# Attention heads in pairs on TensorE: score products that alternate between the row halves of the array, value products between its column halves

## The chip, the cores and the metric

One core of a Trainium2 chip runs the whole program. TensorE (PE, with its weight loads PEld) multiplies, VectorE (DVE) and ScalarE (ACT) do the elementwise work, GpSimd (POOL) builds a few bias tiles, SyncE (SP) issues the weight DMAs. The metric is the device time of one execution in microseconds, lower is better. The profile is of one execution.

## The reference

Four layers over 256 tokens of width 1024, all in float32. Layer 1 mixes pooled channels with causal attention (8 heads of 64), layer 2 is a gated linear recurrence; both are followed by a convolutional feed-forward net. Layers 3 and 4 each have three attention branches over the same tokens, merged by gates, then a feed-forward net and a per-layer embedding. Cut to the attentions:

```python
# layer 1: 8 heads, causal, ALiBi distance (256 tokens are one block, so topk == 0)
logit = einsum('bhqd,bhkd->bhqk', q, k) * scale - slopes * dist      # masked where dist < 0
out = einsum('bhqk,bhkd->bhqd', softmax(logit), v)
# layers 3 and 4
o_mla  = softmax(q @ k.T * scale) @ v                    # 8 heads, q and k 96 wide, v 64 wide
a      = softmax(s[:, 0]) - lam * softmax(s[:, 1])       # 4 heads, two maps each, 64 wide
o_diff = rms_norm(a @ v)                                 # v 128 wide
o_win  = softmax_with_sink(q @ k.T, |q - k| <= 128) @ v  # 8 query heads on 2 key heads, 64 wide
```

## The kernel before

All 256 tokens stay in SBUF as two tiles of 128 tokens; weights stream in chunks of up to 1 MB (three buffers), and ACT and DVE cut each chunk into two exact halves (`hi`, line 258, and `lo`, line 259). The large products run in three passes over these halves (`mm3`, lines 275 to 277); they are the "main products" below, and take nearly all of TensorE. Attention itself is computed in plain float32: each such matmul shows as two MATMUL records, each with its own weight load.

The order of instructions on each engine comes from a list scheduler: it places every instruction by its dependencies and its own estimates, so main products of other work (the gates, the merge) are placed between the steps of a head. Each engine then runs its list in order, and waits for a semaphore where an operand is late.

One head goes through this chain. Scores: two matmuls of 256 columns, one for each half of the queries, into a bank of tag S (two buffers; lines 478 and 479 in layer 1, line 827 else). Softmax: DVE adds a bias and takes the maximum (line 842 or 846), ACT takes the exponential and its sum (line 850), DVE the reciprocal (line 854), ACT normalises (line 859). Transposes on TensorE into a bank of tag T (line 486 or 807), ACT copies them out (line 488 or 809). Value product: two accumulating matmuls with a 64-column weight into half of a bank of tag O (one buffer; lines 490 and 491, or 974 in `pv64`). Two heads share such a bank, one in partitions 0 to 63 and one in 64 to 127, and lines 307 and 308 read it when both are in.

The heads of layer 1, of the differential branch and of the window branch are 64 wide, and two of them lie above each other in one tile: their score matmuls use rows 0 to 63 or rows 64 to 127 of the array. MLA scores use 96 rows. Before, the code finishes one head of a pair ahead of the next; in the differential branch it takes both maps of a head (m = 0 and 1, the same row half) and then the other head:

```python
for e in range(2):                                     # diff
    rr = slice(e * 64, e * 64 + 64)
    for m in range(2):
        sp = self.scores(qk[m][rr, :S], qk[m][rr, S:])
        es.append(self.softmax(sp, FULL, bias))
```

Of the kernel before, what the change touches and what calls it, by code (L numbers as in the profile page):

```python
# [19 lines left out]
P = 128  # L20
S = 256
# [17 lines left out]
# ---------------------------------------------------------------- host: layout only  # L39
# [157 lines left out]
# ---------------------------------------------------------------- device  # L197
class InOrder:
    """An engine whose instructions stay behind those traced before them on it."""
# [9 lines left out]
class Net:  # L209
# [11 lines left out]
    # ---- tiles  # L221
# [22 lines left out]
    # ---- weight stream  # L244
# [27 lines left out]
    # ---- products, three passes over exact halves  # L272
# [6 lines left out]
    def tm_block(self, banks, n, xh, xl, nk, per):  # L279
        """banks[t][:, :n] = x[t] @ W[:, n columns], W in chunks of `per` k tiles."""  # L280
        for k0 in range(0, nk, per):
            wh, wl = self.chunk(per, n)
            for t in range(2):
                for k in range(per):
                    kk = k0 + k
                    self.mm3(banks[t][:, :n], xh[:, kk, t * P:t * P + P], xl[:, kk, t * P:t * P + P],
                             wh[:, k, :], wl[:, k, :], kk == 0, kk == nk - 1)

    def tm_wide(self, banks, xh, xl, kk, last):
        """adds two k tiles into banks[t][n] (1024 columns)."""  # L290
        wh, wl = self.chunk(2, D)
        for n in range(2):
            for t in range(2):
                for k in range(2):
                    self.mm3(banks[t][n][:, :], xh[:, k, t * P:t * P + P], xl[:, k, t * P:t * P + P],
                             wh[:, k, n * 512:n * 512 + 512], wl[:, k, n * 512:n * 512 + 512],
                             kk + k == 0, last and k == 1)
# [12 lines left out]
    # ---- small arithmetic  # L310
    def rsqrt(self, m, n, out=None):
        """1/sqrt of m [P, n] (m > 0)."""
        v = self.nc.vector
        i = self.t([P, 16], "ty", I32)
        v.tensor_scalar(i[:, :n], m.bitcast(I32), -0.5, float(0x5F3759DF), op0=ALU.mult, op1=ALU.add)
        y = i[:, :n].bitcast(F32)
        t = self.t([P, 16], "ty")
        for it in range(3):
            r = self.t([P, 16], "ty") if it < 2 or out is None else out
            v.tensor_tensor(out=t[:, :n], in0=y, in1=y, op=ALU.mult)  # L320
            v.scalar_tensor_tensor(t[:, :n], t[:, :n], -0.5, m, op0=ALU.mult, op1=ALU.mult)
            v.scalar_tensor_tensor(r[:, :n], t[:, :n], 1.5, y, op0=ALU.add, op1=ALU.mult)
            y = r[:, :n]
        return y
# [6 lines left out]
    # ---- residual stream  # L331
# [5 lines left out]
    def norm(self, gi, banks=None, update=None):  # L337
        """Adds banks to x. Leaves halves of the transpose of x * gain, and 1/rms of x
        per token in self.r [P, 2]."""
# [30 lines left out]
    def norm_rows(self):  # L370
        """self.rb [P, S]: 1/rms of the tokens along the free axis."""
        nc = self.nc
        dg = self.t([P, 2, P], "w2")
        pb = self.bank("T")
        for t in range(2):
            nc.scalar.activation(dg[:, t, :], self.ident, AF.Copy, scale=self.r[:, t:t + 1])
            nc.tensor.matmul(pb[:, t * P:t * P + P], self.ones, dg[:, t, :], start=True, stop=True)
        self.rb = self.t([P, S], "rb")
        nc.scalar.activation(self.rb, pb[:, :S], AF.Copy)
# [6 lines left out]
    # ---- head norms in token-major  # L386
    def headnorm(self, z, nh, d):
        """rms-normalises the heads of z [P, 2, nh*d] in place."""
# [21 lines left out]
    # ---- start  # L410
# [19 lines left out]
    def vprod(self, a, b, s):  # L430
        """a * b * s of per-partition vectors."""
        r = self.t([P, 1], f"vp{self.n}")
        self.vec_o.scalar_tensor_tensor(r, a, s, b, op0=ALU.mult, op1=ALU.mult)
        return r

    # ---- block A, layer 0: pooling and causal attention
    def pool_attn(self):
# [33 lines left out]
        for c in range(4):  # L471
            ob = self.bank("O")
            for e in range(2):
                h = 2 * c + e
                r0 = e * 64
                sp = self.bank("S")
                q, k = qT[r0:r0 + 64, c, :], kT[r0:r0 + 64, c, :]
                nc.tensor.matmul(sp[:, 0:P], q[:, 0:P], k[:, 0:P], start=True, stop=True)
                nc.tensor.matmul(sp[:, P:384], q[:, P:S], k, start=True, stop=True)
                bias = self.t([P, 384], "qk")  # L480
                nc.gpsimd.tensor_scalar(bias, causal, -(2.0 ** -(h + 1)), None, op0=ALU.mult)
                s, r = self.softmax(sp, spans, bias)
                self.normalise(s, spans, r)
                pt = self.bank("T")
                for j in range(3):
                    nc.tensor.transpose(pt[:, j * P:j * P + P], s[:, j * P:j * P + P], self.ident)
                pT = self.t([P, 384], "pT")
                nc.scalar.activation(pT, pt[:, :384], AF.Copy)
                vc = slice(h * 64, h * 64 + 64)
                nc.tensor.matmul(ob[r0:r0 + 64, 0:S], v[:, 0, vc], pT[:, 0:S], start=True, stop=False)  # L490
                nc.tensor.matmul(ob[r0:r0 + 64, P:S], v[:, 1, vc], pT[:, S:384], start=False, stop=True)
            self.split(ah[:, c, :], al[:, c, :], ob[:, :S])
# [27 lines left out]
    # ---- feed-forward nets  # L520
    def conv(self, src, wname, bname, j, taps, shifts):
        """depthwise convolution along tokens of src [P, S]."""
# [12 lines left out]
    def fm_first(self, xh, xl):  # L535
        """the first two pairs, k tiles 0-3 of all before k tiles 4-7."""
# [16 lines left out]
    def times_r(self, z, src):  # L553
        """z [P, 2, S] = two banks' or one bank's tiles times 1/rms of the tokens."""
# [56 lines left out]
    # ---- block A, layer 1: gated linear recurrence  # L611
    def softplus(self):
        """-4 and 2 times softplus(-lambda) per channel [P, NR]."""
# [24 lines left out]
    def after(self, ins, group):  # L638
        """ins is issued behind all of group (same engine)."""
# [4 lines left out]
    def rglru(self, gi):  # L644
# [20 lines left out]
        for jp in range(5):  # L665
# [3 lines left out]
            for e in range(2):  # L669
# [5 lines left out]
                # r = (1 + tr) / 2, i = (1 + ti) / 2, w = 4 softplus (1 + tr) = -log a  # L675
# [7 lines left out]
        # sqrt(1 - a^2) = (1 + a) sqrt(tanh(w / 2))  # L683
# [18 lines left out]
    # ---- block B  # L702
# [52 lines left out]
    def layer_scalars(self, i):  # L755
        """minus lambda of the differential attention, rope tables with gains, gain products."""
# [29 lines left out]
    def rope(self, a1, a2, n, shape):  # L786
        """rotates a1, a2 in place."""
# [13 lines left out]
    def transpose4(self, p):  # L801
        """p [P, 2(t), 256 keys] -> [P keys, 2(key block), 256 queries] in SBUF."""
# [9 lines left out]
    def qk_T(self, q, k, d, gain):  # L812
        """q, k: per t APs [P tokens, d] -> [d, q 256 | k 256]."""
# [9 lines left out]

    def scores(self, qT, kT):
# [3 lines left out]
        return sp  # L828

# [5 lines left out]
    def softmax(self, sp, spans, bias=None, sink=None):  # L835
        """exp(scores + bias - max) [P, 512] and 1/sums [P, 2]; sink: (value, -value)."""
# [61 lines left out]
    def mla_heads(self, ch, cl, kr, skr):  # L898
        nc = self.nc
        v_ = nc.vector  # L900
        # queries
# [22 lines left out]
        # keys and values  # L924
# [28 lines left out]
    def mla(self, q4, k4, v):  # L953
# [3 lines left out]
        for cc in range(4):  # L957
            ob = self.bank("O")
            for e in range(2):
                h = 2 * cc + e  # L960
                qk = self.qk_T([q4[:, t, h, :] for t in range(2)], [k4[:, t, h, :] for t in range(2)], 96, self.gm)
                sp = self.scores(qk[:96, :S], qk[:96, S:])
                s, r = self.softmax(sp, FULL)
                self.pv64(ob, e * 64, s, r, v[:, :, h * 64:h * 64 + 64])
# [3 lines left out]
    def pv64(self, ob, r0, s, r, v):  # L968
        """ob[r0:r0+64, queries] = (s / sums) @ v, transposed."""
        nc = self.nc  # L970
        self.normalise(s, FULL, r)
        pT = self.transpose4(s)
        for kb in range(2):
            nc.tensor.matmul(ob[r0:r0 + 64, :S], v[:, kb, :], pT[:, kb * S:kb * S + S], start=kb == 0, stop=kb == 1)  # L974
# [13 lines left out]
    def diff(self, z, v):  # L988
        nc = self.nc
        o = self.t([P, 2, 512], "w4")  # L990
        for hp in range(2):
            qk = []
            for m in range(2):
                cs = slice((2 * m + hp) * P, (2 * m + hp) * P + P)
                qk.append(self.qk_T([z[0][:, t, cs] for t in range(2)], [z[1][:, t, cs] for t in range(2)], P, self.gd))
            for e in range(2):
                h = 2 * hp + e
                rr = slice(e * 64, e * 64 + 64)
                es = []
                bias = self.bias(self.dist, self.slopes(8 + h))  # L1000
                for m in range(2):
                    sp = self.scores(qk[m][rr, :S], qk[m][rr, S:])
                    es.append(self.softmax(sp, FULL, bias))
                (e0, r0), (e1, r1) = es
# [46 lines left out]
    def window(self, i, q, kT, v, oh, ol, heads):  # L1051
        nc = self.nc
        for c in heads:
# [5 lines left out]
            ob = self.bank("O")  # L1059
            for g in range(2):  # L1060
                h = g * 4 + c
                rr = slice(g * 64, g * 64 + 64)
                sp = self.scores(qT[rr, :], kT[rr, :])
                s, r = self.softmax(sp, FULL, self.bias(self.distw, self.slopes(h)),
                                    (self.row(f"sink{i}", 8)[:, h:h + 1], self.negsink[:, h:h + 1]))
                self.pv64(ob, g * 64, s, r, v[:, :, g * 64:g * 64 + 64])
# [12 lines left out]
    def hybrid(self, i, g0):  # L1079
# [54 lines left out]
        # per-layer embedding  # L1134
# [68 lines left out]
```

## Time and profile before

| | |
|---|---|
| median of 3 runs | 1552.79 us (1552.57 to 1553.59) |
| span of the profiled execution | 1551.6 us, 1.2 us under that median |
| TensorE busy | 1532.8 us |
| VectorE / ScalarE busy | 1138.5 us / 941.2 us |
| attention of layer 1 | about 48 to 75 us |
| attention of layers 3 and 4 | about 660 to 803 us and 1140 to 1278 us |

A record of a matmul holds its whole passage through the array, so records overlap and their durations add up to more than the time that they cost: what a group of matmuls costs is read from the starts of the records around it. "Cost of a cluster" below means the time from the start of the last main product ahead of a group to the start of the second main product behind it, less two ordinary pitches of main products.

### The profile page before, as it was taken

The page shows a single profiled execution, that of the slowest core. Times are in us where ns is not written, and L with a number is a line of the kernel's source. Part 1 is how long each engine was busy: PE and PEld are TensorE (multiplying, and loading weights), DVE is VectorE, ACT ScalarE, POOL GpSimd, SP SyncE. Part 2 cuts the span into 40 slices and gives each one's busy share as a digit, 9 for nine tenths or more (in the row PEclk, how much of TensorE's full clock was granted, in tenths as well). Part 3 has the DMA queues.
Part 4 walks back from the last instruction along what each step waited for, and adds up shares of the span by engine and source line. Part 5 has one row for each costly group of instructions (what it writes and reads, how often), then busy time and mean ns, then how long its engine had stood idle before and what let it go on. Part 6 is the DMA issues. An engine that isn't in the chain of part 4 may idle for free.

```text
span 1551.6 us, 25326 instructions
## 1 busy us (share of the span) xinstructions
PE 1532.8 (99%) x10020; PEld 1368.8 (88%) x10020; DVE 1138.5 (73%) x2189; ACT 941.2 (61%) x1675; POOL 51.9 (3%) x45
## 2 busy tenths in 40 slices
PE   8999999999999999999999999999999999999998
PEld 6689999898999998888888999988888889999996
DVE  6559777789897778865767766668885757777666
ACT  6746555685765556756665655566766774655544
POOL 0200000000000000000220000000000210000000
PEclk9999999999999999999999999999999999999999
DMA  8355455435455554533224555544542225455551
GB/s 298 133 178 191 170 192 187 163 136 191 139 214 190 190 178 146 215 132 114 102 103 169 191 191 179 178 173 166 180 179 109 99 86 190 169 186 188 191 188 56
DMA packets 37878, 257.33 MB, mean 166 GB/s; under 512 B 4384, under 2 KB 4768, under 8 KB 8320
## 3 DMA queue, kind: packets, MB, share of 16 engines
q1 hardware_dynamic: 36864, 252.45, 46.0%
q0 software_dynamic: 896, 3.28, 0.7%
q8 instruction: 78, 1.28, 0.3%
q14 instruction: 40, 0.33, 0.1%
HBM read 254.66 MB, written 1.05 MB: 165 GB/s over the span
## 4 chain that ended last, share of the span: by engine, by line
PE 91%; DVE 5%; ACT 2%; issue 1%; DMA 0%; SPq 0%; ACTq 0%; DVEq 0%
PE A L276 14%; PE A L277 13%; PE A L275 13%; PE S L277 6%; PE S L276 6%; PE S L275 6%; PE T L277 6%; PE T L276 5%; PE T L275 5%; PE S L827 2%; PE O L275 2%; PE O L276 2%; PE O L277 2%; PE O L974 2%; DVE lo L259 2%; PE T L807 1%
## 5 line engine op out<-in xcount | busy, mean ns | idle before, releaser
L259 DVE TENSOR_TENSOR lo<-st,hi 128x1024 fp32r<-128x1024 f32 (+2 forms) x480 | 572.2, 1207 | 173.3 <-ACT hi L258 170.6
L258 ACT ACTIVATE hi<-st 128x1024 fp32r<-128x1024 f32 (+2 forms) x480 | 488.8, 1042 | 236.1 <-PE T L276 110.0
L277 PE MATMUL S<-xh,lo 128*128 128x256 f32 x752 | 214.1, 285 | 0.0
L276 PE MATMUL S<-xl,hi 128*128 128x256 f32 x752 | 213.2, 283 | 0.0
L275 PE MATMUL S<-xh,hi 128*128 128x256 f32 x752 | 211.8, 282 | 0.0
L277 PE MATMUL T<-xh,lo 128*128 128x256 f32 x704 | 200.4, 285 | 0.0
L276 PE MATMUL T<-xl,hi 128*128 128x256 f32 x704 | 199.7, 284 | 0.0
L275 PE MATMUL T<-xh,hi 128*128 128x256 f32 x704 | 198.9, 282 | 0.0
L276 PE MATMUL A<-xl,hi 128*128 128x256 f32 x496 | 143.9, 291 | 1.2 <-DVE xl L359 1.1
L275 PE MATMUL A<-xh,hi 128*128 128x256 f32 x496 | 143.6, 291 | 0.0
L275 PEld LDWEIGHTS S<-xh,hi 128*128 128x128 f32 x752 | 142.6, 190 | 0.1
L277 PE MATMUL A<-xh,lo 128*128 128x256 f32 x496 | 142.2, 287 | 0.0
L277 PEld LDWEIGHTS S<-xh,lo 128*128 128x128 f32 x752 | 142.1, 189 | 0.1
L276 PEld LDWEIGHTS S<-xl,hi 128*128 128x128 f32 x752 | 141.6, 188 | 0.0
L275 PEld LDWEIGHTS T<-xh,hi 128*128 128x128 f32 x704 | 133.4, 190 | 1.6
L276 PEld LDWEIGHTS T<-xl,hi 128*128 128x128 f32 x704 | 132.5, 188 | 1.5
L277 PEld LDWEIGHTS T<-xh,lo 128*128 128x128 f32 x704 | 133.0, 189 | 0.1
L275 PE MATMUL A<-hi,xh 128*128 128x512 f32 (+2 forms) x336 | 129.4, 386 | 0.6 <-ACT xh L358 0.6
L276 PE MATMUL A<-lo,xh 128*128 128x512 f32 (+2 forms) x336 | 128.5, 383 | 0.5 <-DVE lo L259 0.5
L277 PE MATMUL A<-hi,xl 128*128 128x512 f32 (+2 forms) x336 | 127.7, 382 | 0.0
L276 PE MATMUL A<-lo,hg 128*128 128x512 f32 x294 | 116.2, 395 | 0.4 <-DVE lo L259 0.4
L275 PE MATMUL A<-hi,hg 128*128 128x512 f32 x294 | 116.2, 395 | 0.0
(347 smaller groups left out, 3012.1 us busy)
## 6 DMA issues: line engine op xcount, KB each, us to landing
st<-in_w_dram SPq DMA_DIRECT2D x230, 1024.0 KB, 4.8
st<-in_w_dram SPq DMA_DIRECT2D x4, 832.0 KB, 4.5
st<-in_w_dram SPq DMA_DIRECT2D x2, 768.0 KB, 5.0
x<-in_x_dram SPq DMA_DIRECT2D x2, 512.0 KB, 4.3
st<-in_w_dram SPq DMA_DIRECT2D x4, 256.0 KB, 7.1
st<-in_w_dram SPq DMA_DIRECT2D x2, 512.0 KB, 3.5
w<-in_gain_dram POOLq DMA_DIRECT2D x2, 512.0 KB, 4.0
out_dram<-x SPq DMA_DIRECT2D x4, 256.0 KB, 2.0
```

Source lines behind the costliest of these rows:

```text
L258: nc.scalar.activation(hi[:, c0:c1], st[:, c0:c1], AF.Copy)
L259: nc.vector.tensor_tensor(out=lo[:, c0:c1], in0=st[:, c0:c1], in1=hi[:, c0:c1].bitcast(F32), op=ALU.subtract)
L275: mm(out, ah, bh, start=start, stop=False)
L276: mm(out, ah, bl, start=False, stop=False)
L277: mm(out, al, bh, start=False, stop=stop)
L807: nc.tensor.transpose(pt[:, kb * S + t * P:kb * S + t * P + P], p[:, t * S + kb * P:t * S + kb * P + P], self.ident)
L827: self.nc.tensor.matmul(sp[:, t * S:t * S + S], qT[:, t * P:t * P + P], kT, start=True, stop=True)
L974: nc.tensor.matmul(ob[r0:r0 + 64, :S], v[:, kb, :], pT[:, kb * S:kb * S + S], start=kb == 0, stop=kb == 1)
```

## The change

Heads are taken in pairs. Both heads' score matmuls are written alternately (second head, first head, second head, first head: rows 64 to 127, rows 0 to 63, ...), then both softmaxes, then both heads' transposes, then both heads' value matmuls alternately (columns 64 to 127, columns 0 to 63, ...). A helper `chained` gives the scheduler an order for the four matmuls of a group; it does not forbid other matmuls between them. MLA scores keep the form of before, only their value products alternate. In the differential branch the value products (128 columns wide) keep their form, and both heads' scores of map 0 now come ahead of both heads' scores of map 1. Number and shape of the matmuls stay the same.

```diff
+    def chained(self, mms):
+
+        last = None
+        for out, lhsT, rhs, start, stop in mms:
+            ins = self.nc.tensor.matmul(out, lhsT, rhs, start=start, stop=stop)
+            if last is not None:
+                self.after(ins, [last])
+            last = ins
...
+    def scores2(self, qk):
+
+        qT, kT = qk
+        sps = [self.bank("S") for _ in range(2)]
+        mms = []
+        for t in range(2):
+            for e in (1, 0):
+                rr = slice(e * 64, e * 64 + 64)
+                mms.append((sps[e][:, t * S:t * S + S], qT[rr, t * P:t * P + P], kT[rr, :], True, True))
+        self.chained(mms)
+        return sps
...
-        self.normalise(s, FULL, r)
-        pT = self.transpose4(s)
+    def pv2(self, ob, probs, vs):
+
+        pTs = []
+        for s, r in probs:
+            self.normalise(s, FULL, r)
+            pTs.append(self.transpose4(s))
+        mms = []
         for kb in range(2):
-            nc.tensor.matmul(ob[r0:r0 + 64, :S], v[:, kb, :], pT[:, kb * S:kb * S + S], start=kb == 0, stop=kb == 1)
+            for e in (1, 0):
+                mms.append((ob[e * 64:e * 64 + 64, :S], vs[e][:, kb, :], pTs[e][:, kb * S:kb * S + S], kb == 0, kb == 1))
+        self.chained(mms)
```

In the differential branch:

```diff
+            for m in range(2):
+                sps = self.scores2((qk[m][:, :S], qk[m][:, S:]))
+                both.append([self.softmax(sps[e], FULL, biases[e]) for e in range(2)])
```

In the window branch:

```diff
+            sps = self.scores2((qT, kT))
+            probs = []
...
-                sp = self.scores(qT[rr, :], kT[rr, :])
...
-                self.pv64(ob, g * 64, s, r, v[:, :, g * 64:g * 64 + 64])
...
+            self.pv2(ob, probs, [v[:, :, g * 64:g * 64 + 64] for g in range(2)])
```

Layer 1 has the same two loops written out in `pool_attn`.

How the scheduler places it is seen in TensorE's list of instructions. In the rows below A is the bank of a main product, T of transposes, S of scores, O of a value product; pT holds transposed probabilities, wv the values, qk and wkT queries and keys.

TensorE in layer 3, the value products of the second window pair, before:

```order
L275 MATMUL A_1261_8322<-xh_838_6093,hi_1253_8205 128x256
L807 MATMUL T_1166_7472<-ident_2_62,s_1164_7461 128x128 x3
L276 MATMUL A_1261_8322<-xl_839_6094,hi_1253_8205 128x256
L974 MATMUL O_1155_7430<-pT_1161_7452,wv_978_6757 64x256 x2
L1056 MATMUL T_1168_7483<-ident_2_62,w_5_996_6854 128x128
L974 MATMUL O_1155_7430<-pT_1167_7477,wv_978_6757 64x256 x2
L1056 MATMUL T_1168_7483<-ident_2_62,w_5_996_6854 128x128
```

Now:

```order
L276 MATMUL A_1256_8262<-xl_839_6094,hi_1246_8143 128x256
L277 MATMUL A_1256_8262<-xh_838_6093,lo_1247_8144 128x256
L838 MATMUL O_1155_7430<-pT_1167_7475,wv_978_6757 64x256
L838 MATMUL O_1155_7430<-pT_1165_7466,wv_978_6757 64x256
L838 MATMUL O_1155_7430<-pT_1167_7475,wv_978_6757 64x256
L838 MATMUL O_1155_7430<-pT_1165_7466,wv_978_6757 64x256
```

The two matmuls of one head stood together, with a transpose between the heads; now the four stand in a row and alternate between the two column halves (pT_1167 belongs to columns 64 to 127).

TensorE in layer 3, the scores of the third window pair, before:

```order
L277 MATMUL A_1261_8322<-xh_838_6093,lo_1254_8206 128x256
L275 MATMUL A_1261_8322<-xh_838_6093,hi_1253_8205 128x256
L827 MATMUL S_1171_7489<-wkT_1069_7124,qk_1169_7486 128x256 x2
L827 MATMUL S_1177_7514<-wkT_1069_7124,qk_1169_7486 128x256 x2
L276 MATMUL A_1261_8322<-xl_839_6094,hi_1253_8205 128x256
L277 MATMUL A_1261_8322<-xh_838_6093,lo_1254_8206 128x256
```

Now:

```order
L838 MATMUL O_1155_7430<-pT_1165_7466,wv_978_6757 64x256
L838 MATMUL S_1172_7490<-wkT_1069_7124,qk_1169_7486 128x256
L838 MATMUL S_1171_7489<-wkT_1069_7124,qk_1169_7486 128x256
L838 MATMUL S_1172_7490<-wkT_1069_7124,qk_1169_7486 128x256
L838 MATMUL S_1171_7489<-wkT_1069_7124,qk_1169_7486 128x256
L275 MATMUL A_1256_8262<-xh_838_6093,hi_1246_8143 128x256
```

Before, both matmuls of one head are followed at once by both of the other; now they alternate, and stand right behind the value products of the pair before.

TensorE in layer 3, the first score group of the differential branch, before:

```order
L276 MATMUL A_1243_8089<-o_1007_6884,hi_1233_7965 128x256
L827 MATMUL S_1076_7145<-qk_1072_7132 128x256 x2
L827 MATMUL S_1079_7155<-qk_1074_7140 128x256 x2
L277 MATMUL A_1243_8089<-o_1006_6883,lo_1234_7966 128x256
L275 MATMUL A_1243_8089<-o_1006_6883,hi_1233_7965 128x256
```

Now, the scores of map 1 (those of map 0 stand nine main products ahead, four in a row):

```order
L277 MATMUL A_1221_7842<-xh_838_6093,lo_1214_7726 128x256
L275 MATMUL A_1221_7842<-xh_838_6093,hi_1213_7725 128x256
L838 MATMUL S_1084_7168<-qk_1074_7140 128x256
L276 MATMUL A_1221_7842<-xl_839_6094,hi_1213_7725 128x256
L277 MATMUL A_1221_7842<-xh_838_6093,lo_1214_7726 128x256
L275 MATMUL A_1221_7842<-xh_838_6093,hi_1213_7725 128x256
L838 MATMUL S_1083_7167<-qk_1074_7140 128x256
L838 MATMUL S_1084_7168<-qk_1074_7140 128x256
L838 MATMUL S_1083_7167<-qk_1074_7140 128x256
L276 MATMUL A_1221_7842<-xl_839_6094,hi_1213_7725 128x256
```

Before, two maps of one head follow each other (banks S_1076 and S_1079, both on rows 0 to 63). Now the group of map 1 is cut by three main products behind its first matmul; the same cut stands in all four groups of map 1 in layers 3 and 4.

## Rows read from the trace of the kernel before

**Rows 1.** The page: busy us of each engine, and the chain.

```profile
PE 1532.8 (99%) x10020; PEld 1368.8 (88%) x10020; DVE 1138.5 (73%) x2189; ACT 941.2 (61%) x1675; POOL 51.9 (3%) x45
...
PE 91%; DVE 5%; ACT 2%; issue 1%; DMA 0%; SPq 0%; ACTq 0%; DVEq 0%
```

**Rows 2.** Busy us by stage: PE, PEld, DVE, ACT, POOL, clock, DMA, GB/s.

```profile
40.00:75.00 35.00, 35.00 (x174) 23.73 (x173) 18.06 (x62) 26.69 (x70) 7.86 (x7) 1.00 0.38 139
660.00:720.00 60.00, 59.74 (x439) 53.71 (x438) 35.89 (x72) 37.16 (x79) 0.00 (x0) 1.00 0.35 123
```

**Rows 3.** PE by time around one MLA value product: start us, us.

```profile
676.61 0.28 PE L275 MATMUL A<-xh,hi 128*128 128x256 f32 x1
676.73 0.28 PE L276 MATMUL A<-xl,hi 128*128 128x256 f32 x1
676.94 1.08 PE L974 MATMUL O<-pT,w 128*64 128x256 f32 x4
677.95 0.39 PE L277 MATMUL A<-xh,lo 128*128 128x256 f32 x1
678.17 0.28 PE L275 MATMUL A<-xh,hi 128*128 128x256 f32 x1
```

**Rows 4.** PE by time, differential scores, same row half twice.

```profile
733.37 0.28 PE L276 MATMUL A<-o,hi 128*128 128x256 f32 x1
733.57 1.99 PE L827 MATMUL S<-qk 64*128 64x256 f32 x8
...
735.72 0.28 PE L276 MATMUL A<-o,hi 128*128 128x256 f32 x1
```

**Rows 5.** PE by time, window scores of two heads back to back.

```profile
756.94 1.14 PE L827 MATMUL S<-wkT,qk 64*128 64x256 f32 x8
...
782.99 0.28 PE L275 MATMUL A<-xh,hi 128*128 128x256 f32 x1
783.20 1.14 PE L827 MATMUL S<-wkT,qk 64*128 64x256 f32 x8
...
784.49 0.28 PE L277 MATMUL A<-xh,lo 128*128 128x256 f32 x1
...
1269.35 1.14 PE L827 MATMUL S<-wkT,qk 64*128 64x256 f32 x8
```

**Rows 6.** PE by time, window scores of two heads apart.

```profile
1231.85 1.13 PE L827 MATMUL S<-wkT,qk 64*128 64x256 f32 x4
1232.90 1.16 PE L1015 MATMUL O<-w,pT 128*128 128x128 f32 x8
1233.99 1.13 PE L827 MATMUL S<-wkT,qk 64*128 64x256 f32 x4
```

**Rows 7.** PE by time, differential scores that turn to the other half.

```profile
746.13 1.75 PE L827 MATMUL S<-qk 64*128 64x256 f32 x8
747.80 0.38 PE L275 MATMUL A<-o,hi 128*128 128x256 f32 x1
```

**Rows 8.** PE by time, one value product of the pooled block.

```profile
62.94 0.40 PE L275 MATMUL A<-hi,xh 128*128 128x512 f32 x1
63.27 0.65 PE L490 MATMUL O<-pT,w 128*64 128x256 f32 x2
...
64.06 0.50 PE L276 MATMUL A<-lo,xh 128*128 128x512 f32 x1
```

**Rows 9.** Line 974: weight loads, min/median/max ns.

```profile
L974 PEld LDWEIGHTS O<-pT,w x64: 132/137/137, 669.1 to 1205.1; 128*64 128x64 f32 x64
```

**Rows 10.** DVE groups, 725 to 800 us: xcount | busy us, mean ns.

```profile
L846 DVE CUSTOM_DVE_ANT_0 s<-S,bias 128x256 f32<-128x256 f32 x16 | 6.3, 414 | 0.2 <-PE S L827 0.2
```

**Rows 11.** ACT groups, 660 to 720 us: xcount | busy us, mean ns.

```profile
L859 ACT ACTIVATE s<-s,at 128x256 f32<-128x256 f32 x14 | 6.3, 500 | 0.6 <-DVE at L854 0.6
...
L809 ACT ACTIVATE pT<-T 128x512 f32<-128x512 f32 x6 | 3.5, 578 | 0.0
```

**Rows 12.** Line 807, transposes of probabilities: PE idle before, us, times.

```profile
  ACT s L859: 7.1, 18
```

More of the change, by code (lines that the diff above doesn't have):

```diff
@@ L472, in pool_attn @@
             ob = self.bank("O")
-            for e in range(2):
[L474 to L479, printed above, removed]
+            sps = [self.bank("S") for _ in range(2)]
+            mms = []
+            for cols, span in ((slice(0, P), slice(0, P)), (slice(P, S), slice(P, 384))):
+                for e in (1, 0):
+                    rr = slice(e * 64, e * 64 + 64)
+                    mms.append((sps[e][:, span], qT[rr, c, cols], kT[rr, c, 0:cols.stop], True, True))
+            self.chained(mms)
+            probs = []
+            for e in range(2):
                 bias = self.t([P, 384], "qk")
-                nc.gpsimd.tensor_scalar(bias, causal, -(2.0 ** -(h + 1)), None, op0=ALU.mult)
-                s, r = self.softmax(sp, spans, bias)
+                nc.gpsimd.tensor_scalar(bias, causal, -(2.0 ** -(2 * c + e + 1)), None, op0=ALU.mult)
+                s, r = self.softmax(sps[e], spans, bias)
                 self.normalise(s, spans, r)
+                probs.append(s)
+            pTs = []
+            for s in probs:
                 pt = self.bank("T")
@@ L488, in pool_attn @@
                 nc.scalar.activation(pT, pt[:, :384], AF.Copy)
-                vc = slice(h * 64, h * 64 + 64)
-                nc.tensor.matmul(ob[r0:r0 + 64, 0:S], v[:, 0, vc], pT[:, 0:S], start=True, stop=False)
-                nc.tensor.matmul(ob[r0:r0 + 64, P:S], v[:, 1, vc], pT[:, S:384], start=False, stop=True)
+                pTs.append(pT)
+            mms = []
+            for kb in range(2):
+                for e in (1, 0):
+                    r0, h = e * 64, 2 * c + e
+                    mms.append((ob[r0:r0 + 64, kb * P:S], v[:, kb, h * 64:h * 64 + 64], pTs[e][:, (0, S)[kb]:(S, 384)[kb]],
+                                kb == 0, kb == 1))
+            self.chained(mms)
             self.split(ah[:, c, :], al[:, c, :], ob[:, :S])
@@ L828, in scores @@
         return sp
+    def scores2(self, qk):
+        qT, kT = qk
+        sps = [self.bank("S") for _ in range(2)]
+        mms = []
+        for t in range(2):
+            for e in (1, 0):
+                rr = slice(e * 64, e * 64 + 64)
+                mms.append((sps[e][:, t * S:t * S + S], qT[rr, t * P:t * P + P], kT[rr, :], True, True))
+        self.chained(mms)
+        return sps
     def bias(self, dist, slope):
@@ L958, in mla @@
             ob = self.bank("O")
-            for e in range(2):
-                h = 2 * cc + e
+            probs = []
+            for h in (2 * cc, 2 * cc + 1):
                 qk = self.qk_T([q4[:, t, h, :] for t in range(2)], [k4[:, t, h, :] for t in range(2)], 96, self.gm)
-                sp = self.scores(qk[:96, :S], qk[:96, S:])
-                s, r = self.softmax(sp, FULL)
-                self.pv64(ob, e * 64, s, r, v[:, :, h * 64:h * 64 + 64])
+                probs.append(self.softmax(self.scores(qk[:96, :S], qk[:96, S:]), FULL))
+            self.pv2(ob, probs, [v[:, :, h * 64:h * 64 + 64] for h in (2 * cc, 2 * cc + 1)])
             self.split(oh[:, cc, :], ol[:, cc, :], ob[:, :S])
         return oh, ol
-    def pv64(self, ob, r0, s, r, v):
-        nc = self.nc
-        self.normalise(s, FULL, r)
-        pT = self.transpose4(s)
+    def pv2(self, ob, probs, vs):
+        pTs = []
+        for s, r in probs:
+            self.normalise(s, FULL, r)
+            pTs.append(self.transpose4(s))
+        mms = []
         for kb in range(2):
-            nc.tensor.matmul(ob[r0:r0 + 64, :S], v[:, kb, :], pT[:, kb * S:kb * S + S], start=kb == 0, stop=kb == 1)
+            for e in (1, 0):
+                mms.append((ob[e * 64:e * 64 + 64, :S], vs[e][:, kb, :], pTs[e][:, kb * S:kb * S + S], kb == 0, kb == 1))
+        self.chained(mms)
     def slopes(self, h):
@@ L995, in diff @@
                 qk.append(self.qk_T([z[0][:, t, cs] for t in range(2)], [z[1][:, t, cs] for t in range(2)], P, self.gd))
+            biases = [self.bias(self.dist, self.slopes(8 + 2 * hp + e)) for e in range(2)]
+            both = []
+            for m in range(2):
+                sps = self.scores2((qk[m][:, :S], qk[m][:, S:]))
+                both.append([self.softmax(sps[e], FULL, biases[e]) for e in range(2)])
             for e in range(2):
                 h = 2 * hp + e
[L998 to L1004, printed above, removed]
+                (e0, r0), (e1, r1) = both[0][e], both[1][e]
                 rl = self.t([P, 16], "ty")
@@ L1059, in window @@
             ob = self.bank("O")
+            sps = self.scores2((qT, kT))
+            probs = []
             for g in range(2):
                 h = g * 4 + c
-                rr = slice(g * 64, g * 64 + 64)
-                sp = self.scores(qT[rr, :], kT[rr, :])
-                s, r = self.softmax(sp, FULL, self.bias(self.distw, self.slopes(h)),
-                                    (self.row(f"sink{i}", 8)[:, h:h + 1], self.negsink[:, h:h + 1]))
-                self.pv64(ob, g * 64, s, r, v[:, :, g * 64:g * 64 + 64])
+                probs.append(self.softmax(sps[g], FULL, self.bias(self.distw, self.slopes(h)),
+                                          (self.row(f"sink{i}", 8)[:, h:h + 1], self.negsink[:, h:h + 1])))
+            self.pv2(ob, probs, [v[:, :, g * 64:g * 64 + 64] for g in range(2)])
             self.split(oh[:, c, :], ol[:, c, :], ob[:, :S])
```

## Prediction

> **What bounds the kernel now.** I read the page first. TensorE (PE) is busy 1532.8 of 1551.6 us, and the chain that ended last runs through it for 91% [rows 1]. The reader should see that nothing else can be the limit over the whole span: VectorE stands at 73%, ScalarE at 61%. Then I looked at the attention stages, by stretches of time [rows 2]: in the MLA stage of layer 3 PE is busy 59.74 of 60 us, ScalarE 37.16, VectorE 35.89; in the attention of layer 1 PE is full and ScalarE busy 26.69 of 35 us. Main products of other work fill the time between the steps of a head. So a microsecond that PE saves inside an attention stage is a microsecond of the span, as long as softmax still comes in time.
>
> A busy PE says nothing of what a matmul costs, so the prices come from starts, as clusters. A value product of one MLA head is four records. From the main product ahead at 676.73 to the second one behind at 678.17 are 1.44 us; two ordinary pitches (676.61 to 676.73) are 0.24; the head costs 1.20 us [rows 3]. Of these 1.01 us lie between its own start and the next, 0.2 us are entry and exit. Differential scores of two maps, eight records on one row half, cost 735.72 - 733.37 - 0.24 = 2.11 us [rows 4].
>
> The row that matters most is the next one. Window scores of two heads are the same eight records, four on each row half. Where the scheduler put them back to back, they cost 784.49 - 782.99 - 0.24 = 1.26 us [rows 5]. So two row halves already run side by side, though the program then has both matmuls of one head ahead of the other's: the order need not alternate. Seven of the eight window pairs show this 1.07 us from the cluster's start to the next main product, the first at 756.94 and the last at 1269.35. Only one pair is apart, with eight matmuls of another step between [rows 6]: 1.05 us from start to next, twice.
>
> **The change part by part.**
>
> *Window scores.* Seven pairs have nothing to gain. The one apart costs 2 x (1.05 + 0.20) = 2.50 us and becomes 1.26: 1.2 us.
>
> *Differential scores.* In each layer the first half of the stage costs 2 x 2.11 us, from [rows 4]. The second half has a single map (1.25 us), a cluster of eight that turns to the other row half in its middle (1.67 us from start to next [rows 7], 1.87 with entry and exit), and a single map: 4.37 us. Together 8.6 us a layer, 17.2 in all. Now there are eight groups of four matmuls. The four of map 0 stand unbroken: 1.26 us each. The four of map 1 are cut by three main products behind the first matmul. That first matmul is alone: two passes. A pass is (2.11 - 1.25) / 4 = 0.215 us, so it costs 2.11 - 6 x 0.215 = 0.82 us. Of the other three, two overlap and the last follows, 1.26 us. A cut group costs 2.08, about what it did. Sum 4 x 1.26 + 4 x 2.08 = 13.4 us: 3.8 us saved.
>
> *Layer 1 scores.* The scheduler puts other matmuls into the groups of the second to fourth pair, and some pairs of before overlapped by themselves. Going through the list, one group loses some 0.8 us and two win 0.7 each: 0.5 us, with bounds of -1 and +1.5.
>
> *Value products.* This is the large part. Sixteen pairs in MLA and window, 2 x 1.20 = 2.40 us each, and four in layer 1. There a head takes 64.06 - 63.27 = 0.79 us from start to next, entry 63.27 - 62.94 less a pitch of 0.23, exit as above, 0.99 together [rows 8], 1.98 a pair. No row of before shows two column halves next to each other: there is always another matmul between. So their price is unknown and bounded by two rows. If they run one after the other, eight passes cost one entry and exit: 1.20 + 4 x 0.215 = 2.06 us, and 0.34 us a pair is saved, 6.8 us over 20 pairs. If they overlap as the row halves do, a pair costs 1.20 + 0.02 (eight records side by side took 1.07 us, four alone 1.05): 1.22 us. That saves 1.18 x 16 = 18.9 us, and in layer 1 1.98 - 1.00 = 0.98 x 4 = 3.9 us: 22.8 us. I take the overlap. A value product shows the same signs of a divided array as the 64-row scores, which a whole-array product lacks: an extra 0.09 us ahead of it and 0.1 us behind it [rows 3].
>
> On the order of instructions a rule speaks against this. The Trainium skill, "TensorE: Matmul & The Clock Gate", Part 3, says that a weight load overlaps a running matmul only when its row group differs, and that matmuls start and end in program order. Two column halves share all row groups, so by it the second head's loads would wait. The trace does not bear out the second half: the window heads above ran side by side although one head's two matmuls both stood ahead in program order. Nor the first as it is put: loads of the value product, on the same rows, take 132 to 137 ns [rows 9], and four of them and four passes fit into 1.01 us.
>
> The same page gives 2.38 times for three column tiles. As an estimate from that, two halves would run 1.6 times as fast as one after the other, and the 22.8 us would be about 19.
>
> *New waits.* Both heads' softmax must now end before either value product, and PE runs its list in order. At the cut group of the differential branch, the first matmul of map 1 needs the bank of the second head, which VectorE reads last: four passes of 414 ns with their readouts [rows 10], some 2 us from when the first half of the scores is in. PE has only the rest of the scores and nine main products, about 2 us less the wait for the first result: about 0.5 us late. The two value banks of this branch use one buffer with four transposes between, about 0.3 us late. That is 0.8 us in four places, 3 us. In MLA, the second head's transposes stand two or three main products (0.3 us) behind the first's, while ScalarE needs 500 ns for each of its two normalising steps and 578 ns for the copy [rows 11]: 0.3 us a pair, 2.4 us. Layer 1, with ScalarE at 76%, 1 us. The window branch already had both heads in flight. Together 6.4 us. Before, waits of this kind were 7.1 us in 18 places [rows 12], which stay. Bounds: nothing, since the scheduler fills with main products, and twice as much, 13 us. Vector, scalar and weight work and all DMAs keep their count, and lie under PE.
>
> *Sum.* 1.2 + 3.8 + 0.5 + 22.8 - 6.4 = 21.9 us. 1551.6 - 21.9 = 1529.7 us of span; the median of the runs stands 1.2 us above the profiled span: 1531 us.
>
> **The rivals.**
>
> *Column halves do not overlap.* Then the value products bring 6.8 us, and 1.2 + 3.8 + 0.5 + 6.8 - 6.4 = 5.9 us remain: 1547 us. For it: no row of before shows two column halves side by side; each streams 128 rows, where two row halves stream 64 each. Against it: the signs of a divided array above.
>
> *No gain.* By the skill's rule each pass of the second head would also show its weight load. As a mechanism of this kernel: the first load of a value product shows about 0.05 us; if each of eight did, a pair would cost 2.06 + 7 x 0.05 = 2.4 us, what it did. Then 5.5 - 6.4 = -0.9 us: 1553 us. Against it is that loads behind the first are hidden today.
>
> *Softmax takes the place of the matmuls: slower.* There are 24 places where both heads are now waited for (8 MLA, 8 window, 4 differential, 4 layer 1). The gain is 28.3 us, so it is gone when PE waits 28.3 / 24 = 1.2 us more in each. At 1.5 us each it would be 1553 + 8 = 1561 us. For it: ScalarE runs its list in order, and a weight half of 1 us ahead of a normalising step would do it. Against it: 31 to 39 main products (3.7 to 4.6 us) mostly stand between the scores and the first transposes, as many as in the window stage of before, and ScalarE is idle 38% of the MLA stage.
>
> **How the numbers follow.** A measurement of this kernel can tell about 0.2% (3 us) from no change. Forecast with overlap: 0.70, between 1523 (28.3 us, no waits) and 1538 (13 us of waits). No overlap: 0.16, around 1547. No gain: 0.07. Slower: 0.07. The range 1523 to 1548 takes in the first two and leaves out the last two and a little below. Faster by over 0.2% takes the first two, less a little for no overlap with long waits: 0.85. Within 0.2%: 0.08. Slower: 0.07.
>
> **What would show it.** Right: in the new profile an alternating value group of eight records goes from its start to the next main product in about 1.02 us, not 1.87; window scores stay at 1.07; the cut groups of the differential branch show no gain; PE's idle time rises by some 6 us, at the transposes and at the scores of map 1. The prediction is wrong if value groups take twice as long, if the idle time before transposes rises by over 13 us, or if the scheduler's new list moves a wait into another stage.

## The result, and the profile after the change

The changed kernel takes 1529.04 us (median; 1528.84 to 1530.40), the kernel before 1552.90 us on the same chip: a ratio of 0.9848, 95% interval 0.9834 to 0.9862, 24 us or 1.5% faster. The forecast was 1531 us. The profiled execution has a span of 1527.4 us, 24.2 us under that of before.

The page of the changed kernel, busy time of each engine and the chain, beside [rows 1]:

```profile
PE 1505.9 (99%) x10020; PEld 1354.4 (89%) x10020; DVE 1136.1 (74%) x2189; ACT 940.3 (62%) x1675; POOL 53.7 (4%) x45
...
PE 86%; DVE 7%; ACT 4%; issue 2%; DMA 0%; SPq 0%; ACTq 0%
```

TensorE does the same 10020 instructions in 26.9 us less and is still full. Its idle time, span less busy, went from 18.8 to 21.5 us. VectorE and ScalarE do the same work, but their share of the chain has grown.

TensorE by time around one MLA value product of the changed kernel (start us, us), beside [rows 3]:

```profile
686.65 0.28 PE L277 MATMUL A<-xh,lo 128*128 128x256 f32 x1
686.86 1.08 PE L838 MATMUL O<-pT,w 128*64 128x256 f32 x8
687.88 0.42 PE L828 MATMUL T<-ident,w 128*96 128x128 f32 x2
```

This is the main reading. Eight records of two heads take 687.88 - 686.86 = 1.02 us from their start to the next instruction; four records of one head took 1.01 us. The second head is free. All 16 MLA and window pairs show 1.01 to 1.02 us. In layer 1, beside [rows 8]:

```profile
61.71 0.40 PE L277 MATMUL A<-hi,xl 128*128 128x512 f32 x1
62.04 0.87 PE L838 MATMUL O<-pT,w 128*64 128x256 f32 x8
62.84 0.33 PE L491 MATMUL T<-ident,s 128*128 128x128 f32 x1
```

0.80 us for two heads, 0.79 for one before.

Differential scores, beside [rows 4] and [rows 7]: the group of map 0, then that of map 1:

```profile
699.50 1.13 PE L838 MATMUL S<-qk 64*128 64x256 f32 x8
700.57 0.39 PE L276 MATMUL A<-xl,hi 128*128 128x256 f32 x1
...
701.62 0.28 PE L275 MATMUL A<-xh,hi 128*128 128x256 f32 x1
701.83 0.70 PE L838 MATMUL S<-qk 64*128 64x256 f32 x2
702.46 0.39 PE L276 MATMUL A<-xl,hi 128*128 128x256 f32 x1
702.68 0.28 PE L277 MATMUL A<-xh,lo 128*128 128x256 f32 x1
702.80 0.28 PE L275 MATMUL A<-xh,hi 128*128 128x256 f32 x1
703.01 1.13 PE L838 MATMUL S<-qk 64*128 64x256 f32 x6
704.07 0.38 PE L276 MATMUL A<-xl,hi 128*128 128x256 f32 x1
704.29 0.28 PE L277 MATMUL A<-xh,lo 128*128 128x256 f32 x1
```

The whole group takes 1.07 us. The cut one costs 702.68 - 701.62 - 0.24 = 0.82 us for the first matmul and 704.29 - 702.80 - 0.24 = 1.25 us for the other three, 2.07 together.

In the window branch, in two of four pairs of each layer, the next pair's scores stand right behind a value product (beside [rows 5]):

```profile
761.27 1.08 PE L838 MATMUL O<-pT,wv 128*64 128x256 f32 x8
762.28 1.13 PE L838 MATMUL S<-wkT,qk 64*128 64x256 f32 x8
763.35 0.39 PE L275 MATMUL A<-xh,hi 128*128 128x256 f32 x1
```

Sixteen records in 2.08 us, with one entry and one exit for both.

Now the waits. Transposes of probabilities in layers 3 and 4 (xcount | busy us, mean ns | idle time of the matmul queue before them), first in the kernel before, then in the changed one:

```profile
L807 PE MATMUL T<-ident,s 128*128 128x128 f32 x160 | 31.6, 285 | 2.4 <-ACT s L859 2.1
```

```profile
L817 PE MATMUL T<-ident,s 128*128 128x128 f32 x160 | 31.3, 282 | 5.3 <-ACT s L890 4.6 <-DVE s L1043 0.4
```

They rose by 2.9 us. (The 7.1 us of [rows 12] counts the weight-load queue too, so it was no measure of what TensorE loses there.) By time, the longest of them and one in layer 1:

```profile
70.86 0.87 PE L838 MATMUL O<-pT,w 128*64 128x256 f32 x8
72.79 0.70 PE L513 MATMUL A<-w,w 128*128 128x256 f32 x2 [1.06 <-ACT w L403]
...
732.78 0.28 PE L276 MATMUL A<-xl,hi 128*128 128x256 f32 x1
734.01 0.33 PE L817 MATMUL T<-ident,s 128*128 128x128 f32 x1 [0.94 <-ACT s L890]
```

From the starts of all groups of half-array matmuls in both traces, the ledger is this (us). A cluster is costed as in the section on the time before, with two additions: where a single matmul stands between two groups, the interval that both would claim is counted once, and idle time inside a group is left out.

| | before | after | saved | forecast |
|---|---|---|---|---|
| MLA value products | 19.7 | 9.5 | 10.2 | 9.4 |
| window scores and value products | 30.7 | 18.9 | 11.8 | 10.6 |
| differential scores | 17.2 | 13.3 | 3.9 | 3.8 |
| layer 1, scores and value products | 14.7 | 10.7 | 4.0 | 4.4 |
| sum | 82.3 | 52.4 | 29.9 | 28.3 |
| span | 1551.6 | 1527.4 | 24.2 | 21.9 |
| given back | | | 5.7 | 6.4 |
| of it, more idle time | 18.8 | 21.5 | 2.7 | |
| of it, busy intervals elsewhere | | | 3.0 | |

The expectations below use sums in which such intervals stand twice (12.9 us for the window branch, 4.3 for the differential scores).

### The profile page after: what moved, and what is told of

Its sections match the earlier page's. It is cut to its first block, busy times and chain, and to the rows that moved or that the text cites. A ratio compares the mean times of both kernels' runs of the same rounds, so it can differ in the third digit from the quotient of the medians.

```text
span 1527.4 us, 25319 instructions
## 1 busy us (share of the span) xinstructions
PE 1505.9 (99%) x10020; PEld 1354.4 (89%) x10020; DVE 1136.1 (74%) x2189; ACT 940.3 (62%) x1675; POOL 53.7 (4%) x45
## 4 chain that ended last, share of the span: by engine, by line
PE 86%; DVE 7%; ACT 4%; issue 2%; DMA 0%; SPq 0%; ACTq 0%
PE A L276 13%; PE A L275 13%; PE A L277 13%; PE S L276 6%; PE S L277 6%; PE S L275 6%; PE T L277 6%; PE T L276 6%; PE T L275 5%; DVE lo L259 2%; PE O L275 2%; PE O L276 2%; PE O L277 2%; ACT hi L258 1%; PE T L817 1%
```

## The experiments

Theory: the two halves of the array, row halves and column halves alike, work side by side whenever matmuls of both stand next to each other; nearly all of the gain is the value products. Rivals: the halves overlap only if the matmuls alternate in program order; or standing in a row, with one entry and exit for two heads, is what brings the gain; or the scores carry it. A second question is where the given-back 5.7 us are.

| kernel | us, median | ratio to before, 95% |
|---|---|---|
| changed | 1529.04 | 0.9834 to 0.9862 |
| scores head by head | 1526.17 | 0.9813 to 0.9840 |
| value products head by head | 1529.57 | 0.9840 to 0.9866 |
| both head by head | 1526.02 | 0.9813 to 0.9839 |
| scores, first head first | 1527.00 | 0.9819 to 0.9846 |
| one column half for both heads | 1545.52 | 0.9936 to 0.9966 |
| value products alone | 1531.67 | 0.9843 to 0.9876 |
| scores alone | 1546.44 | 0.9942 to 0.9971 |
| window branch alone | 1543.98 | 0.9926 to 0.9955 |
| first head scaled on VectorE | 1531.25 | 0.9842 to 0.9875 |
| both heads scaled on VectorE | 1530.63 | 0.9839 to 0.9869 |

**Value products head by head.** In `pv2`, and likewise in layer 1:

```diff
-        for kb in range(2):
-            for e in (1, 0):
+        for e in (1, 0):
+            for kb in range(2):
```

> Both value matmuls of one head stand ahead of both of the other (columns 64 to 127 twice, then columns 0 to 63 twice), still four in a row; the scores still alternate. Theory (the column halves run side by side in either order, what the change brought is that the four stand together): a group of eight records takes 1.02 us from its start to the next main product, and the time is within 1 us of the changed kernel's 1529.0. Rival (only alternation makes them run side by side): the group takes 1.02 plus up to four passes of 0.215 us, 1.9 us, in 16 pairs, and 0.4 us more in the 4 of layer 1: up to 15 us slower, 1540 to 1544 us.

```profile
686.50 0.28 PE L277 MATMUL A<-xh,lo 128*128 128x256 f32 x1
686.71 1.09 PE L838 MATMUL O<-pT,w 128*64 128x256 f32 x8
687.73 0.42 PE L828 MATMUL T<-ident,w 128*96 128x128 f32 x2
```

1.02 us again, and 1529.57 us. Alternation brings nothing here. In the trace the eight passes start in pairs, 13 ns apart, and from the second on one pair every 0.215 us. If matmuls started strictly in program order, the second head's first pass could not start before the first head's fourth, 3 x 0.215 us later, and by this estimate the group would take 1.02 + 0.64, about 1.65 us.

**One column half for both heads.** The same order, but both heads' results go to partitions 0 to 63:

```diff
-                mms.append((ob[e * 64:e * 64 + 64, :S], vs[e][:, kb, :], pTs[e][:, kb * S:kb * S + S], kb == 0, kb == 1))
+                mms.append((ob[0:64, e * S:e * S + S], vs[e][:, kb, :], pTs[e][:, kb * S:kb * S + S], kb == 0, kb == 1))
```

> Value products: four matmuls in a row as in the changed kernel (head by head), but both heads use the same column half (results in partitions 0 to 63, in two column ranges of the bank), and two copies with two subtractions bring them to their places instead of one each; the result is the same. The scores alternate as in the changed kernel. Theory (the gain comes from two column halves that run side by side): with one half only, a group of eight records takes 1.02 plus four passes of 0.215 us, 1.87, from its start to the next main product, 0.86 more in 16 pairs and about 0.65 in the 4 of layer 1: 1529 plus 16, about 1545 us. Rival (the gain comes from the four standing in a row, with one entry and exit instead of two): the group stays at 1.02 us, 1529 to 1531 us.

```profile
691.02 0.28 PE L275 MATMUL A<-xh,hi 128*128 128x256 f32 x1
691.24 1.94 PE L846 MATMUL O<-pT,w 128*64 128x256 f32 x8
693.11 0.70 PE L854 MATMUL S<-qk 96*128 96x256 f32 x2
```

1.87 us, 1545.52 us: both numbers of the theory. It is the second column half, not the standing in a row, that carries 16 of the 24 us (1545.52 against 1529.57 us with two halves in the same order). The added copies are not what costs the time: the clusters of half-array matmuls alone cost 17 us more than there.

**Scores head by head.** In `scores2`, and likewise in layer 1:

```diff
-        for t in range(2):
-            for e in (1, 0):
+        for e in (1, 0):
+            for t in range(2):
```

> Both score matmuls of one head stand ahead of both of the other (rows 64 to 127 twice, then rows 0 to 63 twice); the value products still alternate. Theory (the two row halves run side by side in either order, as the window pairs of before showed): an unbroken group of eight records still takes 1.06 us from its start to the next main product, and the four cut groups of the differential branch, which are whole in this order, each lose 0.6 to 0.8 us: 1529.0 less 2.5 to 3.2 us, about 1526 us. Rival (only alternating matmuls run side by side): a group of eight takes 1.05 plus four passes of 0.215 us, 1.9 us, 0.85 more in each of 8 window groups, 4 whole differential groups and part of the pooled block: about 11 us slower, 1540 us.

1526.17 us, 2.9 us faster than alternating (1525.30 to 1526.63 against 1528.84 to 1530.40). Whole groups still take 1.07 us, so the rival falls. But the reason for the gain is only partly the expected one. The groups of map 1 are no longer cut, yet they don't take 1.07 us:

```profile
701.23 1.63 PE L838 MATMUL S<-qk 64*128 64x256 f32 x8
702.79 0.39 PE L276 MATMUL A<-xl,hi 128*128 128x256 f32 x1
```

1.56 us: 0.5 us more than a whole group, and only some 0.3 us less than the cut one costs, four times 0.3 in place of 0.6 to 0.8. The trace shows why. The head that stands second in the group starts late, when VectorE has read the last of the scores of map 0:

```profile
701.59 0.08 DVE L877 DVE_READ_ACCUMULATOR2_ANT at<- 128x1 f32 x1
...
701.73 0.18 PEld L838 LDWEIGHTS S<-qk 64*128 64x128 f32 x1
```

This first weight load of the second head waits for VectorE, and in all four groups of map 1 it starts 0.05 us behind the end of that read: its bank comes free only then. Another 1.3 us come from layer 1, where groups are cut less and the 1.06 us wait shown above falls to 0.3; idle time before the transposes falls from 5.3 to 4.5 us.

**Both head by head.** Both edits.

> Scores and value products both head by head, each group of four matmuls together, nothing alternates. Theory: as the kernel with the scores alone head by head, about 1526 us, since alternation brings nothing and the whole differential groups save 2.5 to 3.2 us. Rival (alternation is what makes halves run side by side): both losses add up, 1529 plus 11 plus up to 15 us, 1550 us or more, no better than before the change.

1526.02 us: the two don't add anything to each other. This, or the scores alone head by head, is the fastest version of the study.

**Scores, first head first.** `for e in (0, 1)` in the scores, alternating.

> The alternating scores begin with the first head (rows 0 to 63) instead of the second; all else as in the changed kernel. The groups of map 1 in the differential branch stay cut by three main products, but stand five instead of nine main products behind those of map 0. Theory (a cut costs 0.6 to 0.8 us whichever head begins, and softmax of the first map is what the scores of map 1 wait for): the time is 1529 plus or minus 1.5 us, with up to 0.5 us more wait at each of four cut groups. Rival (the order of the heads decides whether the softmaxes stay ahead of the transposes): idle time before the transposes of the MLA, window and differential pairs changes by 0.5 us in each of some 12 pairs, 6 us either way, 1523 or 1535 us.

1527.00 us, 0.5 us outside the theory's interval and far from either time of the rival. The cut groups of map 1 do wait 0.3 us more each, and with these waits differential scores cost 14.6 us where they cost 13.3; layer 1 gives it back (11.8 to 10.5 us with its waits). The order of the heads moves a microsecond here and there through the scheduler; nothing more follows.

**Value products alone, scores alone.** The two halves of the change, each put on the kernel before.

> Only the value products in pairs, in layer 1, MLA and window; the scores and the order of the maps in the differential branch as before the change. Theory (value products carry most): 20 value groups of eight records still take 1.02 us (0.80 in layer 1); lost are the 4.3 us that the differential scores of the changed kernel save by its trace and 1.2 us for one window pair, less about 1 us of waits: 1529.0 plus 4.5, about 1533.5 us, between 1532 and 1535.5. Rival (pairing the scores is what brings the pairs' softmaxes and so their value products together in time): new waits ahead of the transposes take 5 us or more, 1538 us or above.

> Only the scores in pairs (layer 1, differential, window); each head's value product follows its own transposes as before the change, MLA wholly as before. Theory (scores carry little): 5.5 us saved, less 0 to 3 us of waits: 1552.9 less 2.5 to 5.5, 1547.5 to 1550.5 us. Rival (half or more of the gain is the scores'): 1541 us or below.

21.3 us and 6.5 us. The value products carry most; but both runs beat their intervals, and 27.8 is more than the 24 us of both together. The cluster sums do add: 24.0 + 5.8 = 29.8 against 29.9 us. So it is the given-back part that doesn't: 24.0 - 22.3 = 1.7 us of span with the value products alone, nothing with the scores alone (span 6.8 us shorter), 5.7 us with both. (Spans are of one execution each; by the medians it is 2.7 us, nothing and 6.0.) Part of it is seen in the idle time before the transposes: 3.7 and 2.5 us in these two runs, 5.3 with both, 2.4 before. Each saving is nearly free of waits, and both together bring TensorE to the transposes before softmax is done.

**Window branch alone.**

> Only the window branch of layers 3 and 4 in pairs (its scores and its value products); MLA, the differential branch and layer 1 as before the change. By the trace of the changed kernel its half-array groups cost 12.9 us less than before, and its transposes wait 2.6 us more. Theory (each branch stands by itself, and the waits ahead of the window's transposes come from the window's own pairing): 1552.9 less 10.3, about 1542.5 us, with about 5.9 us of waits ahead of its transposes. Rival (the waits come from the differential branch ahead, whose softmaxes now end together): the waits stay near the 3.4 us of before, 1540 us.

1543.98 us, neither's number, and both were wrong in a part. Clusters fall by 11.2 us, the span by 10.1, the median by 9.0. But idle time before the transposes is 2.8 us, hardly over the 2.4 of before: the window's own pairing alone does not make the waits. Idle time of the whole span is 0.4 us less than before, so what was given back is in busy intervals. Sorting all starts of this trace by the kind of matmul ahead and behind shows a part of it: before, transposes of other tiles than probabilities often stood right beside a half-array group (19 times in either order, now 6); now more of them stand behind a main product (14 times, before 8), five of them with an interval of 0.20 us instead of 0.12. A changeover that two steps shared is paid twice there, some 0.5 us in all. The rest was not taken further.

**Scaling on VectorE.** To see whether ScalarE is what the transposes wait for, on the kernel with both head by head:

```diff
+            if e in on_vector:
+                for t, (a, z) in enumerate(FULL):
+                    self.nc.vector.tensor_scalar(s[:, a:z], s[:, a:z], r[:, t:t + 1], None, op0=ALU.mult)
+            else:
                 self.normalise(s, FULL, r)
```

> On top of the kernel with scores and values head by head (1526.0 us): in the window branch alone, VectorE instead of ScalarE scales the first head's probabilities (two instructions of 0.35 us in place of two of 0.50 in each of 8 pairs). Theory (what the change gave back, waits ahead of the window's transposes, is ScalarE: 8.44 of 9.51 us busy between two such waits in the changed kernel, and its exponentials of the second head stand ahead of the scaling of the first): the waits of over 0.3 us ahead of the window's transposes, 0.75, 0.76, 0.88 and 0.53 in layer 3 start to start with the head-by-head scores, shrink by about 0.4 us each, 8 of them: 1523 us, between 1521.5 and 1524.5. Rival (VectorE, which reads the scores first and has the 1.2 us weight halves in its list, is what is late; another task for it makes it later): no gain or a loss, 1526 to 1529 us.

> As the kernel with the first head's scaling on VectorE, but both heads' scaling on VectorE in the window branch. ScalarE then has 2 us less a pair, about 6.5 of 9.5 us, VectorE 1.4 more, about 7.2. Theory (ScalarE is late): as good as with the first head alone or up to 1 us better, 1522 to 1523 us. Rival (VectorE is late): worse than with the first head alone by 1 to 3 us, 1527 us or more.

1531.25 and 1530.63 us, 5.2 and 4.6 us slower than without. The theory's gain does not come: ScalarE had less to do (39.86 us busy between 725 and 785 us, 43.70 without the edit), and the idle time before the transposes, 4.4 us without the edit, is 4.5 us in the first and 5.9 in the second. The chain of the first, in order of time, shows the wait with a new name:

```profile
755.45 0.20 ACT at L883
...
755.67 0.17 DVE at L884
...
755.87 0.18 DVE at L885
...
756.07 1.15 DVE s L1004 x2
...
757.26 0.55 PE T L817 x3
```

The two scalings on VectorE take 1.15 us here, where 0.7 had been counted on. So the runs show that this move does not help; that ScalarE is not what is late they do not show.

The time of the first kernel went elsewhere, and speaks for the theory of the halves. With the new durations the scheduler put the value products into the middle of the next pair's scores:

```profile
760.30 1.13 PE L838 MATMUL S<-wkT,qk 64*128 64x256 f32 x4
761.36 1.09 PE L838 MATMUL O<-pT,wv 128*64 128x256 f32 x8
762.38 1.13 PE L838 MATMUL S<-wkT,qk 64*128 64x256 f32 x4
763.44 0.39 PE L277 MATMUL A<-xh,lo 128*128 128x256 f32 x1
```

3.14 us instead of 2.08 for the same sixteen records: the two heads' scores no longer touch, and each takes its full time. Four such places are 4.2 us of the 5.2. The second kernel doesn't have this; its half-array clusters cost only 0.4 us more, and of 2.2 us more idle time 1.5 stand before the transposes. The rest was not taken further.

## Why the prediction was right

*Value products overlap.* Right, and this was the step that decided. 1.02 us was forecast for the group and measured; the price of a pair, taken over from row halves, held. It was a choice by likeness, since no row of before showed two column halves side by side. With one half only, the group took the 1.87 us named for that case. The Trainium skill, "TensorE: Matmul & The Clock Gate", Part 3, has loads overlap only across row groups and matmuls start in program order. Neither holds here as it is put: with the halves head by head the group takes 1.02 us, its passes in pairs 13 ns apart. The Trainium skill, "TensorEngine Tiling (Array Packing)", Tiling Modes, says that different tiles can load and multiply in parallel, and lists 128 rows by 64 columns as two tiles. In the same page of the Trainium skill, Overview, Theoretical Speedup, up to 2 times is given for a dimension of at most 64. The runs agree, with 1.87 / 1.02 = 1.83 times; the page would have spoken for the overlap.

*Window scores.* Right that the order need not alternate, and that seven of eight pairs had nothing to gain. The term for the whole branch was 1.2 us too small, mostly because four value groups with scores right behind share one entry and exit: 2.27 us each, where 1.22 + 1.26 had been counted.

*Differential scores.* Right to the hundredth: whole group 1.07 us, cut group 2.07 against 2.08, saved 3.9 against 3.8.

*Layer 1.* The sum saved is 4.0 against 4.4; with the wait of 1.06 us behind the last value product, the mark behind the attention (the first matmul of the pooled projection) comes 3.3 us earlier. The scores were put at +0.5 us and bring nothing: alone they leave that mark within 0.1 us of before, and with value products alone it comes 4.4 us earlier.

*New waits.* The total is near, 5.7 us given back against 6.4; its parts are not what was forecast, so the agreement is chance. No wait appeared at the scores of map 1 (3 us forecast with the value banks), and those before the MLA transposes stayed at a few tenths. The window branch, put at nothing because both heads were already in flight, has the longest ones. Layer 1 has its 1 us, but behind the last value product. Idle time rose by 2.7 us, not some 6. The other 3.0 us are in busy intervals, for which the prediction had no term: by sorted starts some 1 us of it at the differential value products; the remainder was not taken further.

*What makes the window's transposes wait* stays open between the engines: moving the scaling off ScalarE didn't help. In the changed kernel the sum and reciprocal of the softmax (lines 884 and 885) stand behind a weight half on VectorE:

```profile
765.64 1.14 DVE lo L259
766.78 0.56 DVE at L884 x2
767.33 0.21 DVE at L885 x2
...
767.97 1.29 ACT s L890 x3
```

That this is the cause was not tried.

## What to carry to other kernels

Two equal groups of matmuls, one on each half of the array, rows or columns, cost here as much as one of them when they stand next to each other on TensorE's list with their operands ready, in either order; look for the pairs that the schedule keeps apart, since only those have something to gain. The order inside a group matters through what surrounds it: score chains that alternate the halves were 2.9 us slower here than the same matmuls head by head, since by the traces the scheduler cut more of them with other matmuls. And when TensorE's part of a stage shrinks, look at what it shared a changeover with, and at the softmax that it now catches up with: a fifth of the saving was given back this way.

## What the runs showed of the hardware that was not expected

The column halves don't need alternating matmuls, and four passes of one half standing ahead don't delay the other (1.02 us either way, 1.87 us on one half).

The same scaling of 128x256 floats on VectorE took 347 ns in the differential branch of the changed kernel and 542 ns in the window branch of the kernel that moved it there (mean of eight each):

```profile
L1042 DVE TENSOR_SCALAR s<-s,at 128x256 f32<-128x256 f32 x8 | 2.5, 347 | 0.1
```

```profile
L1004 DVE TENSOR_SCALAR s<-s,at 128x256 f32<-128x256 f32 x8 | 4.1, 542 | 0.1
```

The expectation had counted 0.35 us. ScalarE needs 0.50, so there the move was no gain even by itself. The trace shows what goes with it. Of that kernel's sixteen scalings, the ten that take 450 to 771 ns lie for the most part inside a bias multiplication on GpSimd, and the four that overlap nothing on GpSimd take 328 to 354 ns. For the two of the chain above it is this one:

```profile
754.89 3.05 POOL L863 TENSOR_SCALAR bias<-distw 128x512 f32<-128x512 f32 x2 [21.29 <-DVE at L877]
```

The overlap alone does not make a scaling slow: two of the changed kernel, wholly inside such a multiplication, take 0.35 us. A run that keeps the two engines apart was not made.
